# Input tiles ahead of the small loads, squares summed tile by tile on TensorE, and four more places for modulation units, in the opening of a two-layer diffusion trunk

## The chip, the core and the metric

The kernel runs on one NeuronCore of a Trainium2 chip. The core has five engines that run at the same time, each through its own queue of instructions in order: TensorE (PE; its weight loads are listed apart as PEld) multiplies matrices, VectorE (DVE) and ScalarE (ACT) work on elements, GpSimd (POOL) takes a few small operations, and SyncE (SP) issues the transfers between the main memory (HBM) and the on-chip memory (SBUF). TensorE writes its results into eight banks of PSUM. Engines wait for each other through semaphores.

The metric is the device time of one execution in microseconds (us). A profiled execution gives a span, from the first to the last instruction, and a trace of every instruction and transfer. The times given for the kernel itself are of executions on the same kind of chip without that bookkeeping in view; the profiled execution has a time of its own, which is named beside its span.

## The reference, cut to what matters

The program is a trunk of two layers over 256 latent tokens and 256 context tokens of 1024 channels, in fp32. Each layer modulates an RMS-normalised input, projects it, runs a convolution branch and an attention branch, merges them, and adds a gated MLP. The change touches only the beginning of the first layer:

```python
s_lat = jax.nn.silu(c)
s_ctx = jax.nn.silu(c_ctx)
...
mod = (s_lat @ w_ada[l] + b_ada[l])[:, None, :]
sh1, sc1, g1, sh2, sc2, g2 = jnp.split(mod, 6, axis=-1)
mod_c = s_ctx @ w_ada[l] + b_ada[l]
...
h = modulate(rmsnorm(x, norm1_g[l]), sh1, sc1)
hc = modulate(rmsnorm(xc, norm1_g[l]), csh1, csc1)
p = h @ w_in[l]
```

with `rmsnorm(x, g) = x * rsqrt(mean(x * x over channels) + EPS) * g` and `modulate(h, shift, scale) = h * (1 + scale) + shift`. So before the first product with `w_in` three things are needed for each block of 128 channels: the sum of squares over all 1024 channels of each token, the shift and scale of these channels (a product of the two condition vectors with columns of `w_ada`), and the input itself.

## The kernel before

**Layout.** Channels lie on the 128 partitions, tokens along the free dimension. The input is eight tiles `x[0..7]` of 128 channels by 512 tokens (256 latent, then 256 context). Weights come in units of 128 by 1024 fp32 values, 512 KB. A product in fp32 accuracy is made of three products in a faster 32-bit form: a weight unit is split into a rounded high part (ScalarE, line 148) and the remainder (VectorE, line 149), and so is the modulated input `h` (ScalarE line 358, VectorE line 359). `mm3` (lines 166 to 169) and `v_tile` (lines 584 to 591) issue the three products.

**Order of the opening.** The instructions are traced in the order in which they stand in the code, and a planner then places each engine's instructions by that order and by when their inputs should be ready. The transfers on SyncE's queue are issued one after the other; one that waits for its target to come free holds back all behind it.

1. Lines 105 to 117: the condition vectors `cv` and the first part of the parameters `par` are loaded by SyncE; GpSimd makes an identity matrix; ScalarE computes silu of the conditions into `sil`, which pulls in ScalarE's function table.
2. Lines 120 to 125: `busy(28)`, 28 dummy products with the identity (56 instructions), gives TensorE something to do while nothing is there yet.
3. Lines 498 to 501: the eight input tiles are loaded, and `SumSq` (lines 298 to 321) squares each on ScalarE and adds the squares up on VectorE into the tile `ss`; the last square is kept apart as a second part.
4. Lines 595 to 605: `rstd` (lines 328 to 344) sums over the partitions on TensorE: for each of four blocks of 128 tokens and each of the two parts a product of the squares (as weights) with a column of ones, eight in all, line 334. VectorE scales (336), GpSimd raises to the power -1/2 (338), and four transposes (343) spread the result over the partitions in the bank `po`. Between these lie the first modulation products, the first half of the first V weight unit, and `busy(3)` and `busy(4)`.
5. Lines 617 to 638: eight rounds, one for each block k of 128 channels. A round modulates tile k (lines 357 to 359), multiplies it with the V weights (`v_tile`, 12 products of 512 columns, lines 589 to 591), computes the modulation of block k + 1 (`ada_now`), and multiplies tile k - 1 with the first gated weights (`glu0`, six products, lines 167 to 169). A new V unit is loaded for every second k, a new gated unit for every fourth. After the last round comes `qk(0)`, and with it the main projections.

**Modulation units.** `ada_products` (188 to 198) loads two units of `w_ada` for one block and multiplies each with the conditions in four groups of 32 rows, 16 matmuls in all (line 194), into the bank `po`; ScalarE copies them out (202), two transposes turn them (209, bank `pt`), VectorE adds up and adds the bias (211, 213), and `gain` (293) makes the factor.

**Places.** Weight units of every kind are loaded into the tag `raw`, which has four places (lines 134 and 140). The tiles with tag `pT` and `k` (lines 466 and 675), two places each and each 4 KB a partition, belong to the attention, which begins after the eight rounds. Temporary tiles `t` (line 69) have five places.

Of the kernel before, what the change touches and what calls it, by code (L numbers as in the profile page):

```python
# [14 lines left out]
P = 128  # L15
# [3 lines left out]
S = 256  # L19
# [25 lines left out]
def trunk(ctx: ExitStack, tc: tile.TileContext, xt, cvec, wall, wada, params, bias_t, rope_t, out):  # L45
# [13 lines left out]
    def nm(s):  # L59
        uid[0] += 1  # L60
        return f"{s}_{uid[0]}"
# [9 lines left out]
    def small(shape, tag, bufs=2):  # L71
        return tp.tile(shape, F32, tag=tag, bufs=bufs, name=nm(tag))

    def sl(w, i):
        return w[:, i * P : (i + 1) * P]
# [27 lines left out]


    cv = cp.tile([P, KD, 2], F32, name="cv")
    sp.dma_start(cv, cvec)
    par = cp.tile([P, DEPTH * NPAR + KD], F32, name="par")
    sp.dma_start(par[:, :DW], params[:, :DW])
    ident = cp.tile([P, P], F32, name="ident")
    make_identity(nc, ident)  # L110
    one = cp.tile([P, 1], F32, name="one")
# [18 lines left out]

    lastdma = [None]

    def raw_unit(src):
        r = wp.tile([P, UW], F32, tag="raw", bufs=4, name=nm("raw"))
        lastdma[0] = sp.dma_start(r, src)
        return r

# [47 lines left out]

    mods = [cp.tile([P, 6 * KD, 2], F32, name=f"mod{l}") for l in range(DEPTH)]

    def ada_products(l, j, bank):

        ps = psum(bank)  # L190
        for u in range(2):
            r = raw_unit(wada[l, 2 * j + u])
            for g in range(4):
                pe.matmul(
                    ps[32 * g : 32 * g + 32, :S], sil[:, 4 * u + g, :], r[:, g * S : (g + 1) * S],
                    start=u == 0, stop=u == 1,
                )
        return ps

    def ada_rows(ps):  # L200
        ev = tp.tile([P, S], F32, tag="ev", name=nm("ev"))
        act.copy(ev, ps[:, :S])
        return ev
# [66 lines left out]
        yield  # L270
        sums(*late)

    def ada_now(j):
        ev = ada_rows(ada_products(0, j, "po"))
        yield
        ada_sums(0, j, ev)
        gain(0, 1, N1G, j)
# [45 lines left out]
    def sum_squares(n, T):  # L323

        at = tp.tile([P, 512], F32, tag="ss", name=nm("ss"))
        return [SumSq(T, at[:, i * T : (i + 1) * T]) for i in range(n)]

    def rstd(ss, n, bank):

        nt = ss.T // P  # L330
        pt = psum("pt")
        for t in range(nt):
            for i, p in enumerate(ss.parts):
                pe.matmul(pt[:, t : t + 1], sl(p, t), one, start=i == 0, stop=i == len(ss.parts) - 1)  # L334
        red = small([P, nt], "red")
        mid = dve.tensor_scalar(red, pt[:, :nt], 1.0 / n, EPS, ALU.mult, ALU.add)
        rs = small([P, nt], "rs")
        pool.tensor_tensor(rs, red, mhalf[:, :nt], ALU.pow)
        yield mid
        yield  # L340
        pb = psum(bank)
        for t in range(nt):
            pe.transpose(sl(pb, t), rs[:, t : t + 1].to_broadcast([P, P]), ident)
        return pb
# [150 lines left out]
                dve.tensor_tensor(self.ol[j][:, c], po[:, c], self.oh[j][:, c].bitcast(F32), ALU.subtract)  # L495


    (ss0,) = sum_squares(1, 2 * S)
    for k in range(KD):
        sp.dma_start(x[k], xt[k])  # L500
        ss0.add(x[k], k == KD - 1)
    h1 = h_tiles()

    for l in range(DEPTH):
# [5 lines left out]
        with ExitStack() as e1a:  # L510
# [68 lines left out]
            with ExitStack() as e1b:  # L579
# [13 lines left out]
                if l == 0:  # L593

                    pv = [psum() for _ in range(4)]
                    sums = rstd(ss0, D, "po")
                    mid = next(sums)
                    nxt = ada_now(0)
                    next(nxt)
                    with tc.issue_after(mid.ins):  # L600
                        wv, more = wparts(l, U_V)
                    busy(3)
                    finish(nxt)
                    ps = whole(sums)
                    busy(4)
                    pb = tp.tile([P, 512], F32, tag="acc", bufs=2, name="rstd0")
                    wg = None
                    pg0 = [psum("sc") for _ in range(2)]
# [8 lines left out]
                    for k in range(KD):  # L617
# [10 lines left out]
                                sp.dma_start(par[:, DW:], params[:, DW:])  # L628
                                sp.dma_start(rope, rope_t)
                        if k + 1 < KD:  # L630
                            nxt = ada_now(k + 1)
                            next(nxt)
                        v_tile(pv, wv, k, range(0 if k else 2, 4))
                        if k + 1 < KD:
# [445 lines left out]
```

## Time and profile before

| | us |
|---|---|
| median of 3 runs | 1157.24 (1157.13 to 1159.2) |
| the profiled execution | 1160.25 |
| its span | 1158.5 |
| mean granted TensorE clock | 0.995 of full speed |
| busy: TensorE, VectorE, ScalarE, GpSimd | 1142.6, 951.8, 557.6, 24.6 |
| moved from HBM | 184.95 MB, 161 GB/s over the span |
| the largest group: first of three products, L167 | 450.9 in 1328 matmuls |

How to read the rows: a timeline or chain row has its start and its length in us from the span's start, then the engine, the line of the kernel, the operation and its tiles as out<-in; x16 is a count of merged instructions. In brackets stands how long the engine was idle before, and what released it. A row of stretches has the stretch, its length, busy times, the granted clock (1.00 is full speed), the busy share of the transfer engines and GB/s. Matmuls are pipelined: their records overlap, so that a row's length is longer than the time to the next one.

### The profile page before, as it was taken

The page shows a single profiled execution, that of the slowest core. Times are in us where ns is not written, and L with a number is a line of the kernel's source. Part 1 is how long each engine was busy: PE and PEld are TensorE (multiplying, and loading weights), DVE is VectorE, ACT ScalarE, POOL GpSimd, SP SyncE. Part 2 cuts the span into 40 slices and gives each one's busy share as a digit, 9 for nine tenths or more (in the row PEclk, how much of TensorE's full clock was granted, in tenths as well). Part 3 has the DMA queues.
Part 4 walks back from the last instruction along what each step waited for, and adds up shares of the span by engine and source line. Part 5 has one row for each costly group of instructions (what it writes and reads, how often), then busy time and mean ns, then how long its engine had stood idle before and what let it go on. Part 6 is the DMA issues. An engine that isn't in the chain of part 4 may idle for free.

```text
span 1158.5 us, 18238 instructions
## 1 busy us (share of the span) xinstructions
PE 1142.6 (99%) x7006; PEld 978.1 (84%) x7006; DVE 951.8 (82%) x1794; ACT 557.6 (48%) x916; POOL 24.6 (2%) x25
## 2 busy tenths in 40 slices
PE   8999999999999999999999999999999999999997
PEld 7677777788769978888888888998879999999996
DVE  3589999968865899988989588789998799888753
ACT  4356667323243354343344222453677567666541
POOL 0000000100000000000000000000000000000000
PEclk8999999999999999999999999999999999999999
DMA  7852313442681345676755455654435474666561
GB/s 242 302 156 79 96 60 110 127 146 60 229 270 60 99 147 171 205 232 201 237 183 160 130 164 180 202 190 132 142 93 163 142 219 125 212 193 183 186 182 55
DMA packets 54230, 187.17 MB, mean 162 GB/s; under 512 B 6272, under 2 KB 6272, under 8 KB 54144
## 3 DMA queue, kind: packets, MB, share of 16 engines
q1 hardware_dynamic: 54144, 186.02, 51.3%
q8 instruction: 55, 0.90, 0.3%
q14 instruction: 31, 0.25, 0.1%
HBM read 184.95 MB, written 1.05 MB: 161 GB/s over the span
## 4 chain that ended last, share of the span: by engine, by line
PE 75%; issue 17%; DVE 3%; DMA 3%; ACT 2%; POOL 0%; SPq 0%; POOLq 0%; DVEq 0%; ACTq 0%
PE main L167 21%; PE main L169 20%; PE main L168 20%; DMA raw<-in_wall 2%; PE po L488 2%; PE sc L419 1%; PE main L589 1%; PE main L590 1%; PE main L591 1%; DVE wlo L149 1%; PE pt L236 1%; PE sc L169 1%; PE pt L334 1%; PE sc L168 1%; PE sc L167 1%
## 5 line engine op out<-in xcount | busy, mean ns | idle before, releaser
L167 PE MATMUL main<-h,whi 128*128 128x256 f32 (+1 forms) x1328 | 450.9, 340 | 1.1 <-ACT whi L148 1.1
L169 PE MATMUL main<-h,wlo 128*128 128x256 f32 (+1 forms) x1328 | 444.1, 335 | 0.1
L168 PE MATMUL main<-h,whi 128*128 128x256 f32 (+1 forms) x1328 | 442.9, 334 | 0.0
L148 ACT CAST whi<-raw 128x1024 fp32r<-128x1024 f32 (+1 forms) x247 | 255.1, 1035 | 341.7 <-PE main L168 171.5
L149 DVE TENSOR_TENSOR wlo<-raw,whi 128x1024 fp32r<-128x1024 f32 (+1 forms) x247 | 296.3, 1204 | 85.8 <-ACT whi L148 84.1
L167 PEld LDWEIGHTS main<-h,whi 128*128 128x128 f32 x1328 | 249.7, 188 | 36.3 <-issue 7.9
L169 PEld LDWEIGHTS main<-h,wlo 128*128 128x128 f32 x1328 | 249.9, 188 | 28.8 <-DVE wlo L149 0.8
L168 PEld LDWEIGHTS main<-h,whi 128*128 128x128 f32 x1328 | 250.2, 188 | 27.0 <-issue 0.6
L259 DVE SCALAR_TENSOR_TENSOR acc<-raw,sil,acc 128x256 f32<-128x256 f32 (+1 forms) x294 | 143.3, 534 | 1.1
L537 DVE SCALAR_TENSOR_TENSOR cb<-u,par,cb 128x512 f32<-128x512 f32 (+1 forms) x240 | 140.2, 611 | 0.6
L167 PE MATMUL main<-fh,whi 128*128 128x256 f32 (+1 forms) x396 | 127.2, 321 | 0.0
L169 PE MATMUL main<-fh,wlo 128*128 128x256 f32 (+1 forms) x396 | 126.4, 319 | 0.0
L168 PE MATMUL main<-fl,whi 128*128 128x256 f32 (+1 forms) x396 | 126.4, 319 | 0.0
L169 PEld LDWEIGHTS main<-fh,wlo 128*128 128x128 f32 x396 | 74.5, 188 | 5.9
L168 PEld LDWEIGHTS main<-fl,whi 128*128 128x128 f32 x396 | 74.5, 188 | 5.7
L167 PEld LDWEIGHTS main<-fh,whi 128*128 128x128 f32 x396 | 74.5, 188 | 5.7
L859 ACT ACTIVATE t<-main,par 128x512 f32<-128x512 f32 (+1 forms) x82 | 50.7, 667 | 13.4 <-PE main L169 13.4
L860 DVE SCALAR_TENSOR_TENSOR t<-main,par,t 128x510 f32<-128x510 f32 (+1 forms) x82 | 47.5, 614 | 1.9 <-ACT t L859 1.5
L863 DVE SCALAR_TENSOR_TENSOR t<-main,par,t 128x510 f32<-128x510 f32 (+1 forms) x82 | 46.8, 610 | 0.0
L799 DVE SCALAR_TENSOR_TENSOR x<-main,mod,x 128x256 f32<-128x256 f32 x48 | 22.2, 480 | 28.1 <-PE main L169 28.1
L358 ACT ACTIVATE h<-t,mod 128x256 fp32r<-128x256 f32 x56 | 25.3, 501 | 35.7 <-DVE t L357 35.7
L878 ACT CAST fh<-t 128x512 fp32r<-128x512 f32 (+1 forms) x44 | 22.5, 513 | 32.6 <-DVE t L875 31.9
(162 smaller groups left out, 1265.0 us busy)
## 6 DMA issues: line engine op xcount, KB each, us to landing
raw<-in_wall SPq DMA_DIRECT2D x239, 512.0 KB, 4.2
raw<-in_wada SPq DMA_DIRECT2D x96, 512.0 KB, 4.3
bias<-in_bias_t SPq DMA_DIRECT2D x16, 256.0 KB, 3.6
x<-in_xt SPq DMA_DIRECT2D x8, 256.0 KB, 4.7
raw<-in_wall SPq DMA_DIRECT2D x8, 256.0 KB, 6.0
out<-t SPq DMA_DIRECT2D x4, 256.0 KB, 2.5
rope<-in_rope_t SPq DMA_DIRECT2D x2, 256.0 KB, 5.3
par<-in_params SPq DMA_DIRECT2D x1, 352.0 KB, 5.6
```

The costliest lines, as they stand in the source:

```text
L148: act.copy(hi[:, c], r[:, c])
L149: dve.tensor_tensor(lo[:, c], r[:, c], hi[:, c].bitcast(F32), ALU.subtract)
L167: pe.matmul(ps, w[0], xh, start=start, stop=False)
L168: pe.matmul(ps, w[0], xl, start=False, stop=False)
L169: pe.matmul(ps, w[1], xh, start=False, stop=stop)
L259: dve.scalar_tensor_tensor(a, w, c, a, ALU.mult, ALU.add)
L358: act.activation(hi[:, c], y[:, c], AF.Identity, bias=b)
L488: pe.matmul(po[i * HD : (i + 1) * HD, c], self.V[kt][:, h * HD : (h + 1) * HD], pts[i][:, kt - kts[0], :], start=kt == kts[0], stop=kt == ...
L537: dve.scalar_tensor_tensor(cb[j], src, w, cb[j], ALU.mult, ALU.add)
L859: act.activation(c, pv_, AF.Identity, bias=pr(l, FDB + t, 1), scale=w[1])
L860: dve.scalar_tensor_tensor(c[:, :, 1:], pv_[:, :, : S - 1], w[0], c[:, :, 1:], ALU.mult, ALU.add)
L863: dve.scalar_tensor_tensor(c[:, :, : S - 1], pv_[:, :, 1:], w[2], c[:, :, : S - 1], ALU.mult, ALU.add)
```

## The change

Three edits, all in the opening of the first layer.

1. The loads of `cv` and `par` are issued from ScalarE's queue, so that the input tiles stand first in SyncE's.
2. The class `SumSq` and `rstd` stay for later norms, but the first norm no longer uses them. Tiles 0 to 6 are squared by ScalarE, the last one by VectorE. VectorE adds the squares in pairs (0 and 1, 2 and 3, 4 and 5). `sum0` sums each of these three pairs, and the tiles 6 and 7 singly, over the partitions on TensorE as they come: four products with the column of ones each, 20 in all, accumulated in the bank `sums0`. `busy(3)` follows each pair. The part of `rstd` behind the sums becomes the generator `root`. In the first layer's opening `busy(3)` behind the first V unit goes, and `busy(4)` becomes `busy(8)`.
3. `ada_now` gets a function `place`, which hands out the tiles for its two units by turns from `pT` and `k`, so that the 16 units of the eight rounds no longer take places of `raw`.

```diff
-    sp.dma_start(cv, cvec)
+    act.dma_start(cv, cvec)
...
-    sp.dma_start(par[:, :DW], params[:, :DW])
+    act.dma_start(par[:, :DW], params[:, :DW])
...
-    def raw_unit(src):
-        r = wp.tile([P, UW], F32, tag="raw", bufs=4, name=nm("raw"))
+    def raw_unit(src, r=None):
+        r = wp.tile([P, UW], F32, tag="raw", bufs=4, name=nm("raw")) if r is None else r
...
-    def ada_products(l, j, bank):
+    def ada_products(l, j, bank, place=lambda: None):
...
-            r = raw_unit(wada[l, 2 * j + u])
+            r = raw_unit(wada[l, 2 * j + u], place())
...
-    def ada_now(j):
-        ev = ada_rows(ada_products(0, j, "po"))
+    def ada_now(j, place):
+        ev = ada_rows(ada_products(0, j, "po", place))
...
                 pe.matmul(pt[:, t : t + 1], sl(p, t), one, start=i == 0, stop=i == len(ss.parts) - 1)
+        return (yield from root(pt, nt, n, bank))
+
+    def root(pt, nt, n, bank):
         red = small([P, nt], "red")
...
-    (ss0,) = sum_squares(1, 2 * S)
+
+    sums0 = psum("pt")
+
+    def sum0(q, first, last):
+        for t in range(4):
+            pe.matmul(sums0[:, t : t + 1], sl(q, t), one, start=first and t == 0, stop=last, skip_group_check=True)
+
     for k in range(KD):
         sp.dma_start(x[k], xt[k])
-        ss0.add(x[k], k == KD - 1)
+        q = tmp()
+        if k == KD - 1:
+            dve.tensor_tensor(q, x[k], x[k], ALU.mult)
+        else:
+            act.activation(q, x[k], AF.Square)
+        if k >= KD - 2:
+            sum0(q, False, k == KD - 1)
+        elif k % 2:
+            dve.tensor_tensor(q, q, prev, ALU.add)
+            sum0(q, k == 1, False)
+            busy(3)
+        prev = q
...
-                    sums = rstd(ss0, D, "po")
+
+                    places = [0]
+
+                    def place():
+                        places[0] += 1
+                        if places[0] % 2:
+                            return eb.tile([P, UW], F32, tag="pT", bufs=2, name=nm("raw"))
+                        return eb.tile([P, UW], F32, tag="k", bufs=2, name=nm("raw"))
+
+                    sums = root(sums0, 4, D, "po")
                     mid = next(sums)
-                    nxt = ada_now(0)
+                    nxt = ada_now(0, place)
                     next(nxt)
                     with tc.issue_after(mid.ins):
                         wv, more = wparts(l, U_V)
-                    busy(3)
                     finish(nxt)
                     ps = whole(sums)
-                    busy(4)
+                    busy(8)
...
-                            nxt = ada_now(k + 1)
+                            nxt = ada_now(k + 1, place)
```

## The prediction

> **What bounds the kernel now.** First the page: engine totals and slices, to see whether the front can matter at all.
>
> ```profile
> span 1158.5 us, 18238 instructions
> PE 1142.6 (99%) x7006; PEld 978.1 (84%) x7006; DVE 951.8 (82%) x1794; ACT 557.6 (48%) x916; POOL 24.6 (2%) x25
> PEclk8999999999999999999999999999999999999999
> ```
>
> TensorE is busy through the span but for 16 us, so time taken from a TensorE gap comes off the end, and time added to its queue goes on it. The change touches only the stretch up to the first context-and-latent projections. The granted clock is low in the first slice alone. I then read the chain of waits, in order of time, from the first sums to the first V matmul (start, length, what):
>
> ```profile
> 11.84 2.22 PE pt L334 x16
> 14.05 1.86 PE po L194 x16
> 15.91 1.58 PE sc L123 x6
> 17.49 0.43 PE pt L209 x2
> 17.92 0.85 PE po L343 x4
> 18.77 1.62 PE sc L123 x8
> 20.40 0.69 PE main L589 x3
> ...
> 43.62 1.00 PE po L194 x16
> ```
>
> From 11.84 us on the chain is TensorE work, and V starts at 20.40. The same 16 modulation matmuls (L194) take 1.86 us here and 1.00 us at 43.62. What came before, from the timeline (start, length, instruction):
>
> ```profile
> 1.83 8.74 PE L123 MATMUL sc<-ident 128*128 128x128 f32 x56 [1.83 <-POOL ident masks.py:199]
> 11.84 0.38 PE L334 MATMUL pt<-one,ss 128*128 128x1 f32 x2 [1.26 <-DVE ss L320]
> 13.20 0.43 PE L334 MATMUL pt<-one,ss 128*128 128x1 f32 x2
> 0.73 0.38 SPq L106 DMA_DIRECT2D cv<-in_cvec  x1
> 1.17 0.42 SPq L108 DMA_DIRECT2D par<-in_params  x1
> 1.65 3.75 SPq L500 DMA_DIRECT2D x<-in_xt  x8
> 8.83 2.71 ACT L316 ACTIVATE t<-x 128x512 f32<-128x512 f32 x4 [1.01 <-DMA x<-in_xt]
> 9.49 2.29 DVE L320 TENSOR_TENSOR ss<-ss,t 128x512 f32<-128x512 f32 x3 [0.78 <-ACT t L316]
> ```
>
> The warm-up of 28 dummy products (56 instructions) ends at 10.57; TensorE is empty for 1.26 us until VectorE's last addition. A dummy record outlives the start of its successor, so I let the next work begin at 10.4. The stretches with the clock (length, TensorE busy, granted clock, DMA share, GB/s):
>
> ```profile
> 13.30:13.40 0.10, 0.10 (x3) 0.77 1.01 389
> 20.10:20.20 0.10, 0.10 (x3) 0.59 0.01 0
> 1153.25:1153.50 0.25, 0.00 (x0) 0.81 0.00 0
> ```
>
> The clock falls to 0.5 at 13.35, rises at 20.18, and falls again at 1153.40 (each read from the mixed value of its stretch). 20.18 - 13.35 = 6.83 is two steps of 3.41, and 1153.40 lies 334 such steps after 13.35. So decisions fall at 9.94, 13.35, 16.77, 20.18 and 23.6.
>
> Last, the eight rounds of V, first gated products and modulation, up to 66.06. The windows row has length, then busy time of PE, PEld, DVE, ACT, POOL; the others are timeline rows, and two of the chain.
>
> ```profile
> 20.40:66.06 45.66, 44.60 (x271) 30.10 (x271) 24.87 (x61) 18.40 (x37) 0.00 (x0) 1.00 0.83 284
> 24.52 0.64 PE L194 MATMUL po<-raw,sil 128*32 128x256 f32 x8
> 25.62 0.64 PE L194 MATMUL po<-raw,sil 128*32 128x256 f32 x8 [0.46 <-DMA raw<-in_wada]
> 26.36 0.97 PE L589 MATMUL main<-whi,h 128*128 128x512 f32 x3
> 29.72 0.40 PE L168 MATMUL sc<-h,whi 128*128 128x512 f32 x1
> 30.34 0.50 PE L169 MATMUL sc<-h,wlo 128*128 128x512 f32 x1 [0.23 <-DVE wlo L149]
> 39.18 1.21 PE L589 MATMUL main<-whi,h 128*128 128x512 f32 x4 [0.26 <-ACT h L358]
> 44.55 0.50 PE L589 MATMUL main<-whi,h 128*128 128x512 f32 x1
> 50.15 0.50 PE L589 MATMUL main<-whi,h 128*128 128x512 f32 x1
> 21.09 0.23 PE main L590
> 22.64 5.31 DMA raw<-in_wall
> 29.06 1.24 DVE wlo L149
> ```
>
> A round without a wait lasts 50.15 - 44.55 = 5.60 us and holds 18 matmuls of 512 columns (0.23 each). The stage holds seven such rounds and one more set of 18 without modulation: 7 x 5.60 + 18 x 0.23 = 43.4 us against 45.66. So **2.3 us of TensorE waits** lie here. Three have a named cause: 0.46 idle before 25.62 (a modulation unit's data), 0.23 before 30.34 (the subtraction for the first gated weights), 0.26 before 39.18 (an activation). A record of 0.40 outlives its turn of 0.23 by 0.17 and hides that much of each, so they are 0.6, 0.4 and 0.4; another 0.2 or so lies before 26.36, the rest in short turns between kinds of work. After 39.2 the rounds run full.
>
> **The change, part by part.** *x first in the queue.* SyncE loses 0.38 + 0.42 us and two gaps ahead of x, so x is issued 1.65 - 0.73 = 0.92 earlier. VectorE's last addition, which now ends at 9.49 + 2.29 = 11.78, would stand at 10.9 at the latest. The two small loads now cost ScalarE 0 to 0.8 us ahead of its table load. That lies beside TensorE's warm-up, since ScalarE already waits for x (1.01 at 8.83). I take nothing for it.
>
> The Trainium skill (Trainium Kernel Development and Optimization, Key Constraints) says that queues of several engines feed the same 16 DMA engines, and that a second issuer saves only issue time. By it this edit is worth at most those 0.92 us; the trace of before has one issuer and can't show it.
>
> *Sums tile by tile.* Eight sum matmuls (16 instructions) become 20 (40 instructions) with nine dummy products between them (18 instructions), all queued behind the warm-up. The L334 rows give twelve instructions in 13.20 - 11.84 = 1.36 us, 0.113 each at full clock. Dummies took 1.62 / 8 = 0.20 each at half clock, so 0.10 to 0.11 at full. From 10.4: 40 x 0.113 + 18 x 0.11 = 6.5, so the sums end at **16.9, not 14.05**. TensorE now sets this, not x: the 0.92 us is hidden entirely. The sixth square must wait for a place among the five temporary tiles until the first sums are through (11.3); it is ready near 12.0 and wanted only at 15, so that costs nothing.
>
> *What follows the sums.* If the clock stays full: modulation 1.1 (with turn) to 18.0, its copy and the semaphores 0.5, two transposes 0.2, four transposes 0.43 (half of 0.85) to 19.2, and eight dummies (16 x 0.11 = 1.8) in place of seven. Part of these can fill the wait for the copy. The copy's row gives 0.37 of its 0.5. GpSimd's power starts 0.29 us behind the sums and lasts 1.02:
>
> ```profile
> 14.34 1.02 POOL L338 TENSOR_TENSOR rs<-red,mhalf 128x4 f32<-128x4 f32 x1 [12.04 <-DVE red L336]
> 15.98 0.37 ACT L202 COPY ev<-po 128x256 f32<-128x256 f32 x1 [0.60 <-PE po L194]
> ```
>
> The sums at 16.9 give 18.2, before the transposes want it. V starts between 20.45 (all TensorE work end to end: 10.4 + 6.5 + 1.1 + 0.2 + 0.43 + 1.8) and 21.0; I take 20.7, **0.3 us later** than now.
>
> *Places.* The 16 modulation units leave the four raw tiles and alternate over two pT and two k tiles, which attention first writes after 70 us:
>
> ```profile
> 73.47 0.38 ACT L677 ACTIVATE qk<-main 128x256 fp32r<-128x256 f32 x1 [0.77 <-DVE t L672]
> ```
>
> Now the first gated weights are issued behind blocked modulation units, at 22.64; then they need only the release of the first unit, near 18, and land 5.3 later, near 23.5. The named waits (0.6, 0.4, 0.4) go. The second V tile still waits for its modulation's transpose, additions and activation (26.36), so part of the time before it stays unless gated products fill it. From both sides: 2.3 if everything is filled; below nothing, -0.5, if the 1.24 us subtraction for the early weights gets ahead of those additions on VectorE. I take **1.5 us**, next to the 1.4 of the three named waits.
>
> Sum: +0.3 - 1.5 = **-1.2 us**. Against the profiled execution (span 1158.5, 1160.25 with what lies around it) this is 1159.05. The median of before is 1157.24, 3.0 below the profiled one, and I carry the difference over: 1156.0. Work after 66 us is unchanged and full.
>
> **Rivals.** *The clock falls behind the sums.* A sum matmul streams one column. Around the fall at the kernel's end the timeline has:
>
> ```profile
> 1148.51 0.28 PE L169 MATMUL main<-fh,wlo 128*128 128x256 f32 x1
> 1149.83 0.38 PE L334 MATMUL pt<-one,t 128*128 128x1 f32 x2 [0.92 <-DVE t L312]
> 1151.76 0.43 PE L343 MATMUL po<-ident,rs 128*128 128x128 f32 x2 [1.10 <-POOL rs L338]
> ```
>
> The step from 1146.58 to 1149.99 was filled to 1148.6 with matmuls of 256 columns, 60%, and the clock held; the next held sums and two transposes, and it fell. Likewise the step 9.94 to 13.35 held 0.4 us of warm-up, 12%, and 1.5 us of sums, and it fell. If sums count for nothing, the step 13.35 to 16.77 now holds dummies for some 0.8 us, 23%, and the clock falls at 16.77: modulation 1.9 to 18.8, copy 0.5, transposes 0.43 and 0.85 to 20.6, sixteen dummies at 0.20 to 23.8. V starts 3.4 us later; with 1.7 back from places (a later start hides more of the waits) **+1.7, 1158.9**. For it: the 12% step that fell. Against it: TensorE is never empty now, and in that step it was.
>
> *It falls at 13.35 already*, the rival on the slower side. The step 9.94 to 13.35 now holds warm-up and dummies for about 1.6 us, 47%. If the clock asks for more (60% held, 12% did not, nothing between is seen), the remaining 24 sum instructions take 0.22 each (the last four of L334: 14.06 - 13.20 over four) and six dummies 0.20: sums to 19.9. Modulation to 21.9, copy and transposes to 23.7, dummies 1.8 to 3.2 by whether it rises at 23.6: V near 26.4, 6.0 later, less 1.7: **+4.3, 1161.5**. It decides from a threshold above 47%.
>
> The Trainium skill (TensorE: Matmul & The Clock Gate, Part 1) says that a free-running window of 3413 ns decides, and that an idle window lowers the clock and a busy one raises it. The trace agrees on the step (3.41 from the three rows). By its wording, with no idle window left, the clock would stay up and the forecast stands; it gives no share for a window of light work, so it settles neither rival.
>
> *Places bring nothing*: the early subtraction delays the second round as much as the weights come earlier. Then +0.3, **1157.5**.
>
> *All waits filled*: 20.45 and 43.4 give -2.2, **1155.0**. TensorE's own work forbids more here.
>
> **How the numbers follow.** Forecast 0.42; fall behind the sums 0.22; fall at 13.35 0.23; no use of places 0.07; all filled 0.06. The predicted time is 1156.0. Its own range is 1155.0 to 1157.4. Over all cases the range is 1154.3 to 1162: the floor less half a microsecond for the measurement, up to the earliest fall. A measurement can tell 0.2%, 2.3 us (before: 1157.13 to 1159.2), so faster means under 1154.9 and slower over 1159.6. Faster: most of the filled case's scatter and a fifth of the forecast's, with some room for a new order of later work: 0.18. Slower: all of the early fall, a third of the later one's scatter and some of the rest: 0.35. Same: 0.47.
>
> **What would show it.** Right: V's first matmul at 20.5 to 21.0, sums ending near 16.9, granted clock 1.0 from 10 to 21, first gated weights issued near 18, no TensorE wait over 0.5 us between 27 and 40, and the stage to the first main projection 43.4 to 44.5 long. A clock of 0.5 from 16.8 or from 13.4 names the rival. Sums ended by 14 would refute the queue behind the warm-up, and with it the whole front term. A V start before 20.4 would mean that dummies run elsewhere than written.

## The result, and the profile after

| | before | after |
|---|---|---|
| median (runs of one comparison) | 1157.98 (5 runs, 1157.13 to 1160.71) | 1168.21 (5 runs, 1168.12 to 1168.81) |
| ratio | 1 | 1.0083, interval 1.0069 to 1.0096 |
| the profiled execution, its span | 1160.25, 1158.5 | 1168.21, 1166.1 |
| mean granted clock | 0.995 | 0.997 |

The kernel is 0.83% slower: ten microseconds by the medians, 7.6 by the two spans. The difference between these two numbers is that the profiled execution of before was one of its slower ones.

The page of after: the totals and the clock in 40 slices.

```profile
span 1166.1 us, 18321 instructions
PE 1145.4 (98%) x7050; PEld 981.5 (84%) x7050; DVE 950.8 (82%) x1792; ACT 557.2 (48%) x915; POOL 24.9 (2%) x25
PEclk9999999999999999999999999999999999999998
```

TensorE's busy time grew by 2.8 us and the span by 7.6, so 4.8 us are new TensorE gaps. The clock isn't low in any of the first slices. Now TensorE's timeline of after, from its first instruction (start, length, instruction). The sums are L506 here, the dummies L123, modulation L194, V L609 to L611:

```profile
7.34 4.42 PE L506 MATMUL pt<-one,t 128*128 128x1 f32 x20 [7.34 <-DVE t L518]
11.63 9.37 PE L123 MATMUL sc<-ident 128*128 128x128 f32 x68
20.84 0.50 PE L506 MATMUL pt<-one,t 128*128 128x1 f32 x4
21.20 0.92 PE L123 MATMUL sc<-ident 128*128 128x128 f32 x6
21.95 1.84 PE L506 MATMUL pt<-one,t 128*128 128x1 f32 x16
23.73 1.07 PE L194 MATMUL po<-raw,sil 128*32 128x256 f32 x16
24.73 1.60 PE L123 MATMUL sc<-ident 128*128 128x128 f32 x12
26.17 0.38 PE L209 MATMUL pt<-ident,ev 128*128 128x128 f32 x2
26.39 0.60 PE L346 MATMUL po<-ident,rs 128*128 128x128 f32 x4
26.82 0.61 PE L123 MATMUL sc<-ident 128*128 128x128 f32 x4
29.30 0.96 PE L609 MATMUL main<-whi,h 128*128 128x512 f32 x3 [1.87 <-ACT h L361]
```

The first thing on TensorE is not the warm-up but 20 sum instructions: two and a half of the five groups of squares that the code writes behind `busy(28)`. They wait for VectorE's first pair addition (L518), which ends near 7.3, and the warm-up waits behind them: 56 dummy instructions and two of the three `busy(3)` in one row of 68. TensorE, which worked from 1.83 on before, is empty until 7.34. The order of instructions on an engine comes from the planner, and it put work that is written later, with inputs that come late, ahead of work that could start at 1.83.

It costs more than the 5.5 us of emptiness. The sums run at 4.42 / 20 = 0.22 us each, the first dummies at 0.21; both are the prices of half clock, while the granted clock stands at 1.00 in these rows. That column misleads here: the trace's records of the clock begin only with its first rise, at 14.86 in this run and at 6.53 in before, and a stretch without a record reads 1.00. At the rise the dummies go from 0.21 to 0.11 us apart, and more of their records fall into a half microsecond (a record counts in every stretch that it touches):

```profile
14.50:15.00 0.50, 0.50 (x5) 0.50 (x4) 0.00 (x0) 0.04 (x1) 0.00 (x0) 1.00 1.05 418
15.00:15.50 0.50, 0.50 (x7) 0.50 (x7) 0.00 (x0) 0.00 (x0) 0.00 (x0) 1.00 1.01 401
```

So the slow start lasts 7.5 us here (from 7.34), 4.7 before (from 1.83).

Last, the end of the opening on VectorE (first block), and the stage from the first V matmul to the first main projection (in the first row the columns of the prediction's row of stretches):

```profile
26.59 0.17 DVE L211 TENSOR_REDUCE mod<-pt 128x4 f32<-128x16 f32 x1 [0.84 <-PE pt L209]
26.68 0.68 DVE L149 TENSOR_TENSOR wlo<-raw,whi 128x512 fp32r<-128x512 f32 x1
27.28 0.15 DVE L213 TENSOR_TENSOR mod<-mod,par 128x4 f32<-128x4 f32 x1
27.35 0.68 DVE L149 TENSOR_TENSOR wlo<-raw,whi 128x512 fp32r<-128x512 f32 x1
27.95 0.15 DVE L293 SCALAR_TENSOR_TENSOR gain<-mod,par 128x2 f32<-128x2 f32 x1
```

```profile
29.30:73.23 43.93, 43.93 (x270) 30.49 (x271) 24.40 (x60) 17.92 (x36) 0.00 (x0) 1.00 0.72 256
```

Two subtractions for weights (L149), here with halves of units, have slipped between the three short steps that make the factor of the first block. The stage itself lasts 43.93 with TensorE busy throughout.

To set beside these, two rows of before. The 20.40 of the prediction is a row of the chain, which starts a matmul where the dummies' last record ends; in the timeline, as in all V starts from here on, the same matmul starts at 20.13:

```profile
20.13 0.96 PE L589 MATMUL main<-whi,h 128*128 128x512 f32 x3
20.13:66.06 45.93, 44.87 (x273) 30.37 (x273) 25.14 (x62) 18.67 (x38) 0.00 (x0) 1.00 0.83 283
```

The balance in spans: V starts at 29.30 instead of 20.13, 9.2 later; the stage takes 2.0 less (43.93 for 45.93); the main projections start at 73.23 instead of 66.06, 7.2 later. The sums end 23.73 - 13.98 = 9.75 later, by the first modulation matmuls behind them; the way from there to V is 0.6 shorter than in before, where the clock was at half on it.

### The profile page after: what moved, and what is told of

Same layout as the page of the kernel before. It is cut to its first block, busy times and chain, and to the rows that moved or that the text cites. A ratio compares the mean times of both kernels' runs of the same rounds, so it can differ in the third digit from the quotient of the medians.

```text
span 1166.1 us, 18321 instructions
## 1 busy us (share of the span) xinstructions
PE 1145.4 (98%) x7050; PEld 981.5 (84%) x7050; DVE 950.8 (82%) x1792; ACT 557.2 (48%) x915; POOL 24.9 (2%) x25
## 4 chain that ended last, share of the span: by engine, by line
PE 76%; issue 17%; DVE 3%; ACT 2%; DMA 1%; POOL 0%; POOLq 0%; DVEq 0%; ACTq 0%; SPq 0%
PE main L167 21%; PE main L169 20%; PE main L168 20%; PE po L491 2%; PE sc L422 1%; PE main L609 1%; PE main L610 1%; PE main L611 1%; DMA raw<-in_wall 1%; DVE wlo L149 1%; PE sc L123 1%; PE pt L236 1%; PE sc L167 1%; PE po L194 1%; PE sc L168 1%
## 5 line engine op out<-in xcount | busy, mean ns | idle before, releaser
L149 DVE TENSOR_TENSOR wlo<-raw,whi 128x1024 fp32r<-128x1024 f32 (+1 forms) x247 | 296.6, 1204 | 86.3 <-ACT whi L148 84.9
L891 DVE SCALAR_TENSOR_TENSOR t<-main,par,t 128x510 f32<-128x510 f32 (+1 forms) x82 | 46.8, 611 | 0.0
L361 ACT ACTIVATE h<-t,mod 128x256 fp32r<-128x256 f32 x56 | 25.3, 503 | 32.7 <-DVE t L360 32.7
```

The source lines that it names most:

```text
L149: dve.tensor_tensor(lo[:, c], r[:, c], hi[:, c].bitcast(F32), ALU.subtract)
L361: act.activation(hi[:, c], y[:, c], AF.Identity, bias=b)
L891: dve.scalar_tensor_tensor(c[:, :, : S - 1], pv_[:, :, 1:], w[2], c[:, :, : S - 1], ALU.mult, ALU.add)
```

## The experiments

My theory after the result was: **the order on TensorE's queue**, and nothing else, makes the loss. The rivals were the sums' own work on TensorE with the clock that falls behind it, the small loads that now land behind x, and the early weights on VectorE. Each ratio is to the kernel before in the same comparison, whose median was 1157.98 to 1159.2 in all of them. V start and the first main projection are timeline rows of each kernel's profiled execution, one execution each, so they depend on where the clock fell in it.

| kernel | median | ratio | V start | first main |
|---|---|---|---|---|
| before, two profiles | 1157.98 to 1159.2 | 1 | 20.13, 19.28 | 66.06, 65.25 |
| after | 1168.21 | 1.0083 (1.0069 to 1.0096) | 29.30 | 73.23 |
| warm-up first | 1163.43 | 1.0040 (1.0024 to 1.0055) | 24.86 | 68.77 |
| warm-up first, no filling between sums | 1161.01 | 1.0015 (1.0006 to 1.0024) | 21.38 | 66.88 |
| dummies with another operand | 1161.12 | 1.0018 (1.0007 to 1.0029) | 20.39 | 65.22 |
| no warm-up | 1163.70 | 1.0036 (1.0024 to 1.0048) | 23.60 | 68.46 |
| sums alone | 1168.90 | 1.0086 (1.0066 to 1.0106) | 28.09 | 74.90 |
| places alone | 1157.95 | 0.9991 (0.9981 to 1.0002) | 19.82 | 64.56 |
| x first alone | 1157.78 | 0.9992 (0.9984 to 1.0001) | 18.22 | 63.58 |
| x first and places, no sums | 1157.53 | 0.9986 (0.9977 to 0.9994) | 19.41 | 63.97 |
| the same, weights held | 1157.27 | 0.9986 (0.9978 to 0.9995) | 18.93 | 63.23 |
| after, weights held | 1168.21 | 1.0081 (1.0065 to 1.0097) | 29.41 | 73.19 |
| fewer sums, weights held | 1157.91 | 0.9995 (0.9987 to 1.0004) | 19.75 | 64.21 |

### The order mended: warm-up first

```diff
 def busy(n):
...
-            pe.matmul(sl(warm, 0), ident, ident, start=True, stop=True)
+            m = pe.matmul(sl(warm, 0), ident, ident, start=True, stop=True)
+        return m
-    busy(28)
+    warmed = busy(28)
...
-        for t in range(4):
+        with tc.issue_after(warmed.ins):
+          for t in range(4):
             pe.matmul(sums0[:, t : t + 1], sl(q, t), one, start=first and t == 0, stop=last, skip_group_check=True)
```

`issue_after` makes the planner place what stands in it behind the named instruction.

> The changed kernel, with one thing more: TensorE takes the sums only behind the 28 dummy products, as the code is written. Theory (the order is the loss: in the changed kernel TensorE stands empty until 7.34 us, then takes the first sums, then 68 dummy instructions, and only then the other sums): the dummies lie beside the loading again, the sums end near 16.9, V starts at 20.5 to 21.0 and not at 29.3, the stage behind keeps its 43.9, and the time is 8.3 to 8.8 us under the changed kernel, 1159.5 +- 0.7, about 1 to 1.5 under before in profiled spans. Rival A (twenty sums of one column let the clock fall): granted clock 0.5 from 13.4 or 16.8, V at 23.8 to 26.4, 1162 to 1165. Rival B (the order is not it, the sums and dummies themselves are): no change from 1168.

Measured: 1163.43, V at 24.86. TensorE's timeline of this kernel (lines are one or two higher), and the stretches in which the clock falls and rises:

```profile
1.83 8.39 PE L123 MATMUL sc<-ident 128*128 128x128 f32 x56 [1.83 <-POOL ident masks.py:199]
10.06 0.95 PE L508 MATMUL pt<-one,t 128*128 128x1 f32 x8
...
12.44 0.91 PE L123 MATMUL sc<-ident 128*128 128x128 f32 x6
13.19 0.95 PE L508 MATMUL pt<-one,t 128*128 128x1 f32 x8
14.00 0.92 PE L123 MATMUL sc<-ident 128*128 128x128 f32 x6
14.75 2.25 PE L508 MATMUL pt<-one,t 128*128 128x1 f32 x16
16.93 1.93 PE L195 MATMUL po<-raw,sil 128*32 128x256 f32 x16
18.79 2.50 PE L123 MATMUL sc<-ident 128*128 128x128 f32 x10
...
24.86 0.96 PE L611 MATMUL main<-whi,h 128*128 128x512 f32 x3 [1.43 <-ACT h L362]
```

```profile
16.00:16.10 0.10, 0.10 (x3) 0.10 (x2) 0.00 (x0) 0.00 (x0) 0.00 (x0) 0.65 0.84 328
22.80:22.90 0.10, 0.10 (x2) 0.10 (x2) 0.10 (x1) 0.00 (x0) 0.00 (x0) 0.72 1.45 246
```

With the order that the prediction had assumed, the sums end at 16.93, where it had put them (16.9). That one edit of order takes V from 29.30 to 24.86 and 4.8 us off the median. But the clock is at half from 16.03 to 22.86 (each read from the mixed value of its stretch): the prediction's first rival, the fall behind the sums, though 0.7 us earlier than named there, with the last sums still running. Its V start was 23.8; the measured one is 1.1 later, and VectorE's timeline has three subtractions of 0.68 between the short steps that make the factor and the first modulation. The kernel stays slower than before, at a time inside rival A's range: by the ratios, mending the order this way takes back about half of the loss (0.0043 of 0.0083), not all.

### Why the planner chose that order: dummies with another operand

The identity that the dummies read is made by GpSimd in several steps and is there at 1.83; the column of ones is a single fill by VectorE, before 0.92.

```diff
-            pe.matmul(sl(warm, 0), ident, ident, start=True, stop=True)
+            pe.matmul(sl(warm, 0), one.to_broadcast([P, P]), one.to_broadcast([P, P]), start=True, stop=True)
```

> The changed kernel with another operand for the dummy products: a broadcast column of ones, which VectorE fills at 0.8 us, in place of the identity that GpSimd makes. The planner then puts all 28 ahead of the sums by itself. Theory (what put the sums first is that the planner expects the identity later than the first squares; on the chip it is there at 1.8): TensorE starts near 0.9, the warm-up ends near 9.4, the sums end near 15.9, V at 20 to 24 by the clock, time 1158.5 to 1163. Rival (the order of the dummies is not what costs): 1167 or more.

Measured: 1161.12 in the median of 12 runs, 1158.37 to 1163.63; the profiled execution is the fastest of them. Its TensorE timeline:

```profile
0.92 7.97 PE L123 MATMUL sc<-one 128*128 128x128 f32 x56 [0.92 <-DVE one L112]
8.73 0.95 PE L506 MATMUL pt<-one,t 128*128 128x1 f32 x8
...
11.10 0.91 PE L123 MATMUL sc<-one 128*128 128x128 f32 x6
11.86 0.95 PE L506 MATMUL pt<-one,t 128*128 128x1 f32 x8
12.67 0.91 PE L123 MATMUL sc<-one 128*128 128x128 f32 x6
13.42 1.84 PE L506 MATMUL pt<-one,t 128*128 128x1 f32 x16
15.19 0.64 PE L194 MATMUL po<-raw,sil 128*32 128x256 f32 x8
...
20.39 0.97 PE L609 MATMUL main<-whi,h 128*128 128x512 f32 x3 [1.16 <-ACT h L361]
```

Nothing was said of order in this kernel, and the warm-up is first. So the dummies' operand decided. The likeliest reason is the readiness that the planner expects: its order fits an identity that comes later than the first squares, where the chip has it 5.5 us before their sum. The planner's own estimates are not on record, so this reason is argued, not shown. The sums end at 15.19, and in this execution the clock never fell in the opening, so V starts at 20.39 and the main projections at 65.22, 0.8 before those of before. The other runs have no trace, but their mean clock suggests that it does fall in most: the two runs with 0.998 took 1158.37 and 1158.62, the seven with 0.996 or less 1159.99 to 1163.63.

### What the warm-up costs and brings: none

```diff
-    busy(28)
+    busy(0)
```

> The changed kernel without the 28 dummy products; the others stay. Theory (the 56 dummy instructions stand in series between two groups of sums, 7.7 us of the 9.2 that 68 take): V 5 to 7.7 us earlier, 21.6 to 24.3, the smaller gain if the rest then runs at the cold clock throughout; time 1160.5 to 1163. Rival (the dummies cost nothing because the cold clock would make all else slower by as much): V within 1.5 of 29.3, 1167 or more.

Measured: 1163.70, 0.7 above the expected range, and V at 23.60, inside it.

```profile
7.12 4.43 PE L506 MATMUL pt<-one,t 128*128 128x1 f32 x20 [7.12 <-DVE t L518]
11.41 2.91 PE L123 MATMUL sc<-ident 128*128 128x128 f32 x12
```

The 20 early sums still wait for VectorE and are still slow, but 56 dummies behind them are gone: V is 5.7 earlier and the median 4.5 lower. In after the dummies stood on the path, in series. Put first, where the code has them, they gain nothing over none by these medians: that kernel took 1163.43 (1.0040), this one 1163.70 (1.0036), and V starts later there (24.86).

### The sums alone

```diff
-    act.dma_start(cv, cvec)
+    sp.dma_start(cv, cvec)
...
-    act.dma_start(par[:, :DW], params[:, :DW])
+    sp.dma_start(par[:, :DW], params[:, :DW])
...
-            r = raw_unit(wada[l, 2 * j + u], place())
+            r = raw_unit(wada[l, 2 * j + u])
```

> The changed kernel with its two other parts undone: small loads first on SyncE's queue, modulation units in the raw places; the sums tile by tile and the dummies as changed. The planner again puts the first two groups of sums ahead of the 28 dummy products. Theory (the order alone is the loss): TensorE empty until about 7.2, V near 29, and the stage behind it 45 to 45.7 as before, since the places are gone: 1168.5 to 1170.5. Rival (the loss needs x first, by which the first squares overtake the dummies): V near 24 or earlier, at most 1164.

Measured: 1168.90, the same as after. The order is there without the other two edits, only the split of the early sums differs:

```profile
6.72 1.87 PE L506 MATMUL pt<-one,t 128*128 128x1 f32 x8 [6.72 <-DVE t L518]
9.00 1.87 PE L506 MATMUL pt<-one,t 128*128 128x1 f32 x8 [0.41 <-DVE t L518]
10.73 10.25 PE L123 MATMUL sc<-ident 128*128 128x128 f32 x68
```

V starts at 28.09, 1.2 before after's, and the stage lasts 74.90 - 28.09 = 46.8: without the places it has its waits back (1.7 us of TensorE in five of them, the longest 0.73 for a modulation unit). A late start alone doesn't shorten the stage.

### The other two edits, apart and together

Against the kernel before, places alone has this (and `place` itself with the parameters that carry it, as in the change):

```diff
-    def ada_now(j):
-        ev = ada_rows(ada_products(0, j, "po"))
+    def ada_now(j, place):
+        ev = ada_rows(ada_products(0, j, "po", place))
...
-                    nxt = ada_now(0)
+                    nxt = ada_now(0, place)
...
-                            nxt = ada_now(k + 1)
+                            nxt = ada_now(k + 1, place)
```

x first alone has this, and the third kernel both, with the squares summed as before:

```diff
-    sp.dma_start(cv, cvec)
+    act.dma_start(cv, cvec)
...
-    sp.dma_start(par[:, :DW], params[:, :DW])
+    act.dma_start(par[:, :DW], params[:, :DW])
```

> The kernel before with the four more places for modulation units alone. Theory (the parts are independent; places are worth what the changed kernel's stage shows, 43.93 against 45.66 from the first V matmul to the first main projection): V still at 20.4, the stage 43.9 +- 0.3, time 1.7 under before. Rival (the shorter stage comes only from the late start, by which all weights have long landed): the stage stays at 45.3 or more and the time within 0.5 of before.

> The kernel before with only the two small loads moved to ScalarE's queue. Theory (x lands 0.9 earlier, but the condition vectors now land behind it, at 4.0 in place of 2.4, and ScalarE begins its squares 0.8 later): the last addition ends 0.2 to 0.9 before 11.78, V starts up to 0.9 before 20.4, time 0 to 0.9 under before. Rival (the late condition vectors cost more than x gains): 0.2 to 0.8 over before.

> The changed kernel with the sums undone: x first and the places stay, squares are added on VectorE and summed at the end as before, busy(3) and busy(4) as before. Theory (sums and their order cost all, the two other parts gain): V near 20, stage 43.9, time 1.7 to 2.6 under before, and 11 to 13 under the changed kernel. Rival (the parts don't add up: an earlier start brings the waits back that the places took away): within 0.8 of before.

Measured: 0.9991 and 0.9992, both with intervals that reach past 1, and 0.9986 (0.9977 to 0.9994) together. The stage lasts 64.56 - 19.82 = 44.74 with places alone; with both:

```profile
19.41:63.97 44.56, 44.56 (x273) 30.66 (x273) 26.10 (x63) 18.32 (x37) 0.00 (x0) 1.00 0.74 261
```

Places take 1.2 to 1.4 off the 45.93 of before, less than the 2.0 in after and than the theory had; the time falls by 1.2 us (1159.11 to 1157.95), not by 1.7, and isn't clear of none. The rival to that, a shorter stage only by the late start, fails on the sums alone: there the start is late and the stage is 46.8. With x first alone the sums begin at 11.02 instead of 11.84, so 0.82 of the 0.92 earlier issue arrives where TensorE waits; ScalarE's table load comes at 3.71 instead of 2.43, because the condition vectors land behind x, and the first square begins at 5.12 instead of 4.62; the sums come earlier all the same. Its V start of 18.22 owes a part to the clock, which was down for one step of 3.41 in that execution (13.41 to 16.82) and for two in before's first profile. Together the two edits took 1.6 us off the median, just short of the 1.7 to 2.6 expected. They are the first version that is measurably faster than both kernels, by 0.14%.

### No filling between the sums

The kernel with the warm-up first, without the three `busy(3)` in the loop:

```diff
             sum0(q, k == 1, False)
-            busy(3)
```

> The kernel with the sums held behind the warm-up, without the nine dummy products between the sums. Theory (the nine only lengthen the queue by 18 x 0.11 = 2.0 us and do not hold the clock, which fell at 16.1 with them): sums end at 14.8 to 15, the clock falls between 12.5 and 16.5, V 1.5 to 2.5 us earlier than 24.86, time 1.5 to 2.5 under that kernel's 1163.4. Rival (they kept the clock up until 16): the clock falls at 12.7 or before the sums end, sums end after 16, V no earlier than 24.3.

Measured: 1161.01. The sums end near 14.0 instead of 16.9, and V starts 3.5 earlier than with the filling. Then VectorE (first row) and TensorE (second) show the wait that is next:

```profile
19.17 1.23 DVE L150 TENSOR_TENSOR wlo<-raw,whi 128x1024 fp32r<-128x1024 f32 x1 [1.50 <-ACT whi L149]
```

```profile
21.38 1.80 PE L610 MATMUL main<-whi,h 128*128 128x512 f32 x4 [2.10 <-ACT h L362]
```

The factor is ready at 17.7, but the first modulation (L361) stands on VectorE behind a subtraction for weights whose cast on ScalarE is still waiting for the transfer. TensorE is empty for 2.10. The weights that places brought forward are in the way of what is needed first. Without filling, the clock falls too, to 0.50 from 14.9 to 18.3, and behind the empty stretch once more from 21.7 to 25.1, under the first V matmuls.

### The early weights held back

```diff
+                    low0 = []
...
-                            wg = wunit(l, U_GLU0 + k // 4)
+                            with tc.issue_after(low0[0].ins):
+                                wg = wunit(l, U_GLU0 + k // 4)
...
-                            wv = wunit(l, U_V + k // 2, cuts=2)
+                            with tc.issue_after(low0[0].ins):
+                                wv = wunit(l, U_V + k // 2, cuts=2)
...
+                            low0.append(low)
```

Splits of later weights now stand behind the first modulated tile. Once in after, once in the version without the sums:

> The changed kernel, with the subtractions for the weights that now land early held on VectorE behind the first modulated tile; nothing else. Theory (in the changed kernel two of them, 0.6 to 0.7 us each, stand between the first modulation's sum and its gain and delay V): from the first modulation's transposes to V 1.0 to 1.3 us shorter than 3.13 (26.17 to 29.30), V at 28.0 to 28.3; the time 0.8 to 1.3 under the changed kernel, if the stage behind keeps 43.9. Rival (they are hidden, the path runs over GpSimd and the transposes): V within 0.3 of 29.3 and the same time.

> The kernel with x first and places, sums as before, and the same subtractions held behind the first modulated tile. Theory (one subtraction of 1.2 us stood ahead of the low half of the first tile there and TensorE filled the time): V's low products start 0.5 to 1.1 earlier, but the work that filled is now missing elsewhere, so 0 to 0.8 under 1157.5. Rival (holding them makes the first gated weights late again): 0.5 to 1.5 over it.

Measured: 1168.21 and 1157.27, neither different from the kernel without the hold. In the first, from the transposes of the modulation to V:

```profile
11.45 10.61 PE L123 MATMUL sc<-ident 128*128 128x128 f32 x68
...
27.23 0.38 PE L209 MATMUL pt<-ident,ev 128*128 128x128 f32 x2
...
29.41 0.96 PE L609 MATMUL main<-whi,h 128*128 128x512 f32 x3 [0.92 <-ACT h L361]
```

That path takes 29.41 - 27.23 = 2.18 instead of 29.30 - 26.17 = 3.13 in after: the subtractions cost 0.95, where their two rows of 0.68 partly overlap the short steps. But in this execution the 68 dummies took 10.61 instead of 9.37, since the slow start lasted until 17.27, and the gain went under. V began at 29.41, not at the expected 28.0 to 28.3. Whether the other three executions lost it in the same way is open: they have no trace. In the version without the sums the clock stayed at 1.0, TensorE was done with its filling at 16.5, and V still began only at 18.93. ScalarE shows why:

```profile
16.90 1.56 ACT L148 CAST whi<-raw 128x1024 fp32r<-128x1024 f32 x2 [2.42 <-DMA raw<-in_wall]
18.37 0.91 ACT L358 ACTIVATE h<-t,mod 128x256 fp32r<-128x256 f32 x2
```

The activation that makes the first modulated tile stands behind casts of weights, and these wait 2.42 for their transfer. With a full clock the opening's end is set in this execution by the arrival of weights, not by the sums.

### Fewer sums

Against the kernel with the warm-up first: 24 dummies, the squares of tiles 0 to 5 added on VectorE, so that three groups (24 instructions) are left on TensorE, `busy(3)` and `busy(4)` behind, weights held.

```diff
-    warmed = busy(28)
+    warmed = busy(24)
...
-        elif k % 2:
+            continue
+        if k:
             dve.tensor_tensor(q, q, prev, ALU.add)
-            sum0(q, k == 1, False)
-            busy(3)
+        if k == KD - 3:
+            sum0(q, True, False)
```

> x first, places, 24 dummies held ahead of the sums, squares 0 to 5 added on VectorE and summed on TensorE while 6 and 7 still land, then these two singly (12 sum matmuls in place of 20 or 8), busy(3) and busy(4) as before, subtractions held. Theory (TensorE's queue ends the sums, so fewer sum matmuls behind a shorter warm-up let them end with the data): sums end near 12 to 12.5, V at 17.5 to 19.5 by the clock, 0.5 to 1.5 under the kernel with x first and places alone, 2 to 3 under before. Rival (the clock decides: with a shorter warm-up it falls as early or earlier and takes back what is won): within 0.5 of that kernel.

Measured: 1157.91, 0.9995 (0.9987 to 1.0004). The sums end at 13.84, not near 12 to 12.5, and the clock is at half from 12.13 to 18.95. These edits together bring the kernel level with before, but not below the version with before's own sums, as the rival had it.

### The kernel before, profiled again

> The kernel before once more, for its trace alone. Theory (its times of 1156 to 1162.6 come from where in its opening the granted clock falls and for how long): the time at which the clock falls differs from 13.35, in steps that stay 3.41 long, and the span follows it: near 1155.5 if the clock is down for one step, near 1158.5 for two. Rival (the scatter is the loading of the input): the clock falls within 0.3 of 13.35 and rises after two steps whatever the span.

Measured: 1159.28, span 1157.5; the clock fell at 13.76 and rose one step later, at 17.17, where the prediction's execution had lost two steps. V began at 19.28 and the main projections at 65.25, both 0.8 earlier than in the first profile; the stage was the same (46.0 for 45.9), with a wait of 0.92 for the transfer that had cost 0.46. The fall did move, but the size missed: the span lies between the 1155.5 that the theory had for one step down and the 1158.5 for two.

## Why the prediction was wrong

**The step that failed** is the clause "all queued behind the warm-up". The prediction took the order of the code for the order on TensorE, and so let the warm-up run free beside the loading from 1.83 on. The runs showed 20 sum instructions in front, TensorE empty until 7.34, and the 56 dummies in series behind them. The prediction had written down the sign that would refute the order (sums ended by 14, or V before 20.4) for one side only, and none of its rivals was a sum in front of the warm-up. The working from there, taken against V at 20.7:

- *Sums end, 16.9.* Measured 23.73, 6.8 later: work begins 5.5 later (7.34 for 1.83), and the same 114 instructions take 16.4 instead of the 15.1 of the kernel with the warm-up first, 1.3 more, since the slow start runs longer. Behind the warm-up the end came at 16.93. That it agrees to 0.03 is partly luck: the work behind the warm-up began at 10.06, not 10.4, and the last 0.9 us of it ran at half clock. Without that fall the end would be near 16.5 (estimated from these rows), 6.4 behind 10.06, so the size of the term, 6.5, was right.
- *From the sums to V, 3.8.* Measured 5.57. Of the 1.8 more, 0.95 is the two subtractions ahead of the factor (held back, it is 29.41 - 24.79 = 4.62). The other 0.8 was missing in the term itself, which counted TensorE's work end to end: the planner put twelve dummies ahead of the transposes, which start at 26.17 though the copy they need is done at 25.23 (24.86 + 0.37 in ScalarE's timeline), and behind the transposes TensorE waits for VectorE and ScalarE, 1.87 here. With the other operand and a full clock it was 5.20. This part was not tried apart.
- *Places, -1.5.* The stage lasted 43.93 where the prediction had asked for 43.4 to 44.5: -1.73 against its 45.66 from the chain, -2.00 by the timeline's 45.93 (which puts the waits of before at 2.5, not 2.3). Right in after. Where V starts at 19.8 the gain is 1.2; why it is smaller there was not tried. The bound of -0.5, an early subtraction ahead of the additions on VectorE, did come true, but at the first block and outside the stage: 0.95 in after, and a large part of 2.10 without the filling.
- *x first, nothing.* As predicted, hidden in after. In the order of before it brings 0.82 at the sums, but its time (0.9992) can't be told from none.
- *Rivals.* Hidden under the wrong order, the clock that falls behind the sums is real: in the one profile of the mended kernel it falls at 16.03, and the kernel is 4.6 us slower than before by the ratio, not 1.7. The fall at 13.35, which the prediction took as the slower side, wasn't seen there. The forecast itself, a full clock, was met by one profiled execution (another operand): sums at 15.19, V 5.20 behind them, a stage of 44.83, and 1158.37. That is 0.8 below the median of before in its comparison (1159.2), where the forecast had 1.2; but the dummies started 0.9 earlier there than the forecast had them.

The sum closes with these terms, counted as the prediction did (from 20.40): -1.2 predicted, +6.8, +1.8 and -0.2 for the stage make +7.2, the difference of the first main projections.

What the chip shows against the whole edit, with any order tried: the 20 sum matmuls end between 14.0 and 16.9 with the warm-up in front, the eight of before at 12.9 to 13.3 with x first; and the clock fell under the last sums (16.03) or just behind them (14.90) in the two profiles with the warm-up held first. So the loss has at least two parts: the order, and the larger set of sums with the half clock around its end. Only two executions with the mended order have a mean clock of 0.998 (another operand, 1158.37 and 1158.62), too few to divide the second part further. Every kernel with the full set of sums was slower than before (1.0015 to 1.0086), every one without them level or faster. What stays open too is how the 0.14% divides between x first and places, and whether a mended order with other filling could bring the sums below before.

## What to carry to other kernels

Where a planner places instructions, the order on each engine has to be read or forced before anything is costed: a few summing matmuls that it put ahead of a warm-up turned 28 free dummy products into a serial block. Filling work should read the operand that is ready first: with an identity ready at 1.83 other work passed in front of it here, with a column of ones ready at 0.92 none did. Work brought forward (weights, here) has to be followed through every engine that it then passes: the 0.68 us subtractions stood before the first factor.

## What was not expected of the hardware

**Light matmuls and the clock.** The clock fell or stayed for two kernels with the same sums and dummies in the same turn. The kernel with the warm-up first fell at 16.03. The one with another operand sped up near 4.0 and fell only at the end:

```profile
3.50:4.00 0.50, 0.50 (x4) 0.50 (x4) 0.00 (x0) 0.18 (x1) 0.00 (x0) 1.00 1.19 320
4.00:4.50 0.50, 0.50 (x7) 0.50 (x6) 0.00 (x0) 0.50 (x1) 0.00 (x0) 1.00 0.89 291
...
1150.00:1151.00 1.00, 0.14 (x2) 0.00 (x0) 0.83 (x3) 0.00 (x0) 0.00 (x0) 0.94 0.00 0
```

The last row puts its fall at 1150.88, 336 steps of 3.413 (the prediction's rows give (1153.40 - 13.35) / 334) behind 4.0, so its decisions lay at 10.8 and 14.25. Counting the dummies' time alone in the step before each decision, from the timelines: 1.32 of 3.41, 39%, where it fell at 16.03, and 1.51, 44%, where it held at 14.25. If one-column sums counted for nothing, a line would lie between, and the 47% that the prediction feared would hold. But no single share comes out of these traces. The kernel without warm-up fell at 18.17 behind a step with 1.04 of dummies and 0.57 of modulation matmuls, 47% together; x first and places with the weights held kept its clock at 14.55, two steps after its rise at 7.72, behind a step with 0.57 and 1.00, 46%. What the light matmuls count for stays open.

To come up it takes more. In after the step of sums up to 11.44 didn't raise the clock, and the step full of dummies up to 14.86 did; with the weights held in after, a step with 2.41 of dummies (71%) behind sums didn't, up to 13.86; without warm-up a step with 2.70 (79%) did, up to 14.76.

The Trainium skill (TensorE: Matmul & The Clock Gate, Part 1) says that the window runs freely and that the point of change differs from run to run. The trace agrees: in the two profiles of before the clock rises at 6.53 and 6.93 and falls at 13.35 and 13.76. Over all profiles with the sums of before the first fall lies between 12.5 and 13.8 in five, and a sixth has none in the opening (x first and places, weights held).

**How far one kernel scatters by it.** The 79 runs of before that stood beside the experiments took 1155.98 to 1162.58, and their medians by mean granted clock are:

```
clock   runs   median us
0.994     9    1160.47
0.995    27    1159.62
0.996    37    1158.52
0.997     4    1156.60
0.998     2    1158.02
```

From 0.994 to 0.997 the median falls as the mean clock rises, by 4 us; the two runs at 0.998 don't follow. The phase of the clock is a likely part of this scatter, but not shown to be its cause. The two profiles of before differ by one step of half clock and by 1.0 us of span; and x first and places with the weights held took 1158.28 in the one execution whose clock is known not to have fallen in the opening, and 1157.27 in the median of 11. After scatters by 0.7 us in its five runs, with no fall in the opening of its profile; with the weights held it shows no fall either, and four runs scatter by 2.5. So a comparison of a few runs can't tell differences of 1 or 2 us here, whatever the cause.
